# A list scheduler for a fused decoder layer: its step prices are taken from the trace, and steps on other rows than the one ahead get a price

## The chip, the core and the metric

The kernel runs on one core of a Trainium2 chip. A core has five engines with a queue each: TensorE (PE in the profile; its weight loads are PEld), VectorE (DVE), ScalarE (ACT), GpSimd (POOL) and SyncE (SP). Each works its queue in order and waits at semaphores for the others. SBUF and PSUM are memories of 128 partitions ("rows" below); matmuls write PSUM, and ScalarE and VectorE empty it. The metric is the device time of one launch in microseconds, the median of several runs; lower is better.

## The reference

One decoder layer, batch 1, 2048 tokens, width 1024, float32. `h` is the RMS-normalized input; one projection of `h` feeds three branches and their gates.

```python
h = rms_norm(x, norm_g[l])
p = h @ w_in[l]                      # 7552 columns, split into 13 parts
y_a = rwkv7_mix(...) * silu(z_a)     # 8 heads x 64, delta-rule state
y_b = sliding_window_sink_attn(...) * silu(z_b)   # 8 q heads, 2 kv heads x 64, window 128
y_c = memory_cross_attn(...) * silu(z_c)          # 4 heads x 128 over 256 memory tokens
gates = sigmoid(p_gate)              # 3 x 1024 per token
merged = gates_a * (y_a @ w_proj_a) + gates_b * (y_b @ w_proj_b) + gates_c * (y_c @ w_proj_c)
x = x + merged @ w_out
```

The recurrence of branch A is, for each head and token, `S = S * w + (S a) b^T + v k^T` and `y = S r`.

## The kernel before, in words

The 2048 tokens are worked in four stages of 512 (`sb` 0 to 3). All wide products are made in three matmuls of split operands: each float32 operand is split into a high and a low part, and `gemm3` adds high x high, high x low and low x high (lines 457 to 459). A projection block of 128 columns (`proj`) is 8 such triples into one of two PSUM buffers `mm`; a product with a `w_proj` block is 4. The weights are split in stage 0 (lines 439 and 440), written to DRAM, and read back in the stages after (`wblock`).

In each stage two streams are woven together. One (`stream_r`) is branch A, in two groups of two head pairs. `rwkv_prep` makes the chunked operands of a pair (chunks of 64 tokens): decays by a scan (line 697), then many VectorE steps on 64 of the 128 rows, since the two heads of a pair lie on rows 0 to 63 and 64 to 127 (`EV`, `OD`; lines 728, 732, 737, 742), Gram matrices on TensorE (line 753) that VectorE masks (lines 760 and 761), and transposes (line 770). One step of GpSimd (line 724) fills a mask in between. `rwkv_inverse` inverts small triangular matrices on VectorE (lines 803 to 805, 31 times three steps). `rwkv_chain` walks the eight chunks: bursts of small matmuls (lines 866, 867, 874, 859, 881), and between them a copy (line 869), a scaling (878) and the state's update (882) on VectorE, and scaled copies of the state on ScalarE (872). The other stream (`stream_f`) holds branches C and B with their softmaxes (line 1102, an exponential with a running sum), the gates, and two of the three merges. The third merge, the next stage's normalized input and the output product follow.

The order of the instructions in each engine's queue isn't that of the program. When all instructions have been written, `order` hands them to a list scheduler. `Step` gives each instruction a price: `busy`, how long it holds its engine, and `dur`, how long until its result is there. `cost_PE`, `cost_ACT`, `cost_DVE`, `cost_POOL` and `cost_SP` (lines 95 to 132) work these out from the operands. `steps` finds what each step must wait for and gives it a rank, which is its place in the program with a few corrections (weights are moved up to 1000 ahead, steps that read PSUM 600 ahead, the steps of the inverse 500 back). `lay_out` then plays the program with these prices: each time, the engine that can start earliest takes, among its steps that are ready at that moment, the one of least rank. A step counts as ready a fixed allowance after its feeders' ends: for TensorE 200 ns in the recurrence and 600 ns elsewhere (`LAT`, lines 65 to 67). When TensorE's last step had another tile size than the full array, steps of the same size go first. The orders found are fixed as dependencies, and the chip's queues follow them. So the prices reach the chip only through the order of each queue; no arithmetic step is added or removed by them (ScalarE's table loads stand wherever its order changes the set of functions).

Small matmuls that belong together are tied by `together` and are offered as a group.

Of the kernel before, what the change touches and what calls it, by code (L numbers as in the profile page):

```python
# [55 lines left out]
class Step:  # L56


    def __init__(self, ins, masks):
        self.ins, self.eng = ins, NAMES[ins.engine]  # L60
        self.reads, self.writes = ([self.region(a.bass_ap, masks) for a in aps if getattr(a, "bass_ap", None) is not None]
                                   for aps in (ins.ins, ins.outs))
        self.reads, self.writes = ([r for r in l if r] for l in (self.reads, self.writes))
        self.before, self.after, self.opens, self.group, self.end = set(), [], [], [], None
        self.lat = LAT[self.eng]
        if self.eng == "PE" and not any(r[0].startswith(("Z_", "W_", "R_")) or r[0] in ("Z", "W", "R") for r in self.reads):
            self.lat = 600
        self.bytes = 512 * self.n((self.writes + self.reads)[0]) if self.is_dma() else 0
        getattr(self, "cost_" + ("SP" if self.bytes else self.eng))()

# [25 lines left out]
    def cost_PE(self):  # L96
        out, mov, w = self.writes[0], *self.reads[:2]
        n = self.n(out)
        self.tile = tuple(128 if r[3][0][1] > 64 else 64 if r[3][0][1] > 32 else 32 for r in (mov, out))
        self.dense = mov[5] == F32R  # L100
        if self.dense:
            self.busy = 14 + 0.424 * n
        elif self.ins.is_transpose:
            self.busy = 108 if self.tile[0] == 128 else 55
        elif self.tile[1] == 128:
            self.busy = 223 + max(0, n - 128) * 1.7 if self.tile[0] == 128 else 62 + max(0, n - 64) * 0.8
        else:
            self.busy = 32 if self.tile[1] == 32 else max(58, 0.86 * n)
        self.dur = max(270, self.busy + 160)

    def cost_ACT(self):
        r = self.reads[0]
        self.dur = (170 if r[4] else 206) + 0.83 * self.n(r) + 90 * (len(self.reads) - 1 + len(self.writes) - 1)
        self.busy = self.dur - (85 if len(self.writes) > 1 else 38 if r[4] else -12)
        self.table = {AF.Sin: 1, AF.Exp: 2, AF.Tanh: 2}.get(self.ins.func, 0)

    def cost_DVE(self):
        r, two = self.reads[0] if self.reads else self.writes[0], sum(self.n(x) > 1 for x in self.reads) > 1
        slow = two or r[4] or type(self.ins).__name__ not in ("InstTensorScalarPtr", "InstTensorCopy", "InstMemset")
        self.dur = 155 + (1.05 if slow else 0.53) * self.n(r) + 30 * (len(self.reads) - 1)  # L120
        self.busy = max(100, self.dur - 85)
        if two and r[4] and self.n(r) <= 128:
            self.busy = self.dur + 20

    def cost_POOL(self):
        n = self.n(self.writes[0])
# [54 lines left out]
def lay_out(tc, todo):  # L181

    metas = {tag: meta.bufs for p in tc.info.pools if p.space != bass.MemoryType.DRAM for tag, meta in p.tag_meta.items()}
    source = {t.name: t.source_name for t in tc.info.tiles}
    tags = {tag: Tag(b) for tag, b in metas.items()}
    users, opened = {}, set()
    for s in todo:
        for name in {r[0] for r in s.reads + s.writes}:
            users.setdefault(name, []).append(s)
        for r in s.writes:  # L190
            if source[r[0]] in tags and r[0] not in opened:
                opened.add(r[0])
                s.opens.append(r[0])
                tags[source[r[0]]].queue.append(r[0])
    left = {name: len(u) for name, u in users.items()}
    heads = {tag: 0 for tag in tags}
    clock = {e: 0.0 for e in NAMES.values()}
    ready, parked = {e: {} for e in clock}, set()
    orders = {e: [] for e in clock}
    missing = {s: len(s.before) for s in todo}  # L200

    def seen_by(s, b):

        if b.eng == s.eng:
            return 0 if s.eng == "PE" else b.end + 30
        return b.end + s.lat

    def room(s):

        at, taken = 0.0, {}  # L210
        for name in s.opens + [n for g in s.group for n in g.opens]:
            tag = source[name]
            t, i = tags[tag], taken.get(tag, 0)
            if t.queue[heads[tag] + i] != name or len(t.free) <= i:
                return None
            taken[tag] = i + 1
            old = t.free[i]
            if old:
                at = max([at] + [seen_by(s, b) for b in last[old].values()])
        return at  # L220

    def offer(s):
        at = room(s)
        if at is None:
            parked.add(s)
            ready[s.eng].pop(s, None)
        else:
            parked.discard(s)
            ready[s.eng][s] = max([at] + [seen_by(s, b) for b in s.before])

    last = {name: {} for name in users}
    for s in todo:
        if not missing[s]:
            offer(s)
    tile, fp32, wires, table = (128, 128), False, 0, 2
    for _ in todo:
        best = None
        for e, rs in ready.items():
            if rs:
                at = max(clock[e], min(rs.values()))  # L240
                if best is None or at < best[0]:
                    best = at, e
        at, e = best
        can = [s for s, t in ready[e].items() if t <= at]
        s = min(can, key=lambda s: s.rank)
        if e == "PE":
            if tile != (128, 128) and s.tile != tile:
                s = min(can, key=lambda s: (s.tile != tile, s.dense, s.rank))
            if s.tile != tile:
                at += 95  # L250
            clock[e] = at + s.busy
            if s.dense and fp32:
                clock[e] += 95
            elif s.tile != tile and s.tile[1] < 128:
                clock[e] += 49
            tile, fp32 = s.tile, not s.dense
        else:
            if e == "ACT" and not s.bytes and s.table and s.table != table:
                at, table = at + 1280, s.table
            clock[e] = at + s.busy  # L260
        s.end = at + s.dur
        if s.bytes:
            wires = s.end = max(wires, s.end) + s.bytes / 330
        del ready[e][s]
        orders[e].append(s)
        again = set()
        for name in s.opens:
            tag = source[name]
            tags[tag].free.pop(0)
            heads[tag] += 1  # L270
            again.add(tag)
        for name in {r[0] for r in s.reads + s.writes}:
            if e not in last[name] or last[name][e].end < s.end:
                last[name][e] = s
            left[name] -= 1
            if not left[name] and source[name] in tags:
                tags[source[name]].free.append(name)
                again.add(source[name])
        for a in s.after:
            missing[a] -= 1  # L280
            if not missing[a]:
                offer(a)
        if again:
            for a in [a for rs in (parked, *ready.values()) for a in rs if any(source[n] in again for g in [a, *a.group] for n in g.opens)]:
                offer(a)
    return orders


def order(tc, manual, groups):

    orders = lay_out(tc, steps(list(tc.nc.cur_bb.bb.instructions), manual, groups))
    how = mybir.DependencyInfo(mybir.DependencyClass.NoSync, mybir.DependencyReason.DATA)
    for l in orders.values():
        for a, b in zip(l, l[1:]):
            tc.add_manual_dep(b.ins, a.ins.name, how, reason="order")
# [1083 lines left out]
```

## Time and profile before

| | |
|---|---|
| median of 3 runs | 2248.6 us (2247.82 to 2249.54) |
| profiled execution: its own time | 2250.41 us |
| profiled execution: span on the core | 2248.6 us |
| granted TensorE clock, mean | 0.998 |
| instructions in the trace | 36877 |
| TensorE busy | 2219.2 us, 99% |
| VectorE busy | 1531.7 us, 68% |
| ScalarE busy | 926.1 us, 41% |
| GpSimd busy | 149.7 us, 7% |
| DMA | 430.55 MB, mean 191 GB/s |

The span runs from the first to the last instruction of the program. A row of a group ("x1888 | 750.0, 397 | 1.5 <-DVE gt L928 1.5") gives the number of instructions, their busy time in microseconds, the mean length of one in nanoseconds, the engine's idle time just ahead of them, and who ended it. A row of the timeline gives start, length (of all, where several are merged), engine, line, operation, output and inputs, and in brackets the idle time ahead. Matmuls overlap, so the distance between two starts tells their pace, and not their length. Steps of ScalarE and VectorE overlap a little too: the next one often starts before the last has ended.

### The profile page before, as it was taken

Reading aid. Unit: us, or ns where it says so; the run is one execution under the profiler, and the core shown is the slowest. Engines: PE = TensorE matmul, PEld = TensorE weight load, DVE = VectorE, ACT = ScalarE, POOL = GpSimd, SP = SyncE. Lnnn points to the kernel's source line nnn. Section 1 sums busy time; section 2 is a strip of 40 time slices with the busy share of each in tenths; the row PEclk is TensorE's granted clock in tenths of the full one; section 3 lists DMA queues with packets and bytes.
Section 4 is the critical chain, followed back from the end, with each engine's and each line's share of the span. In section 5 each row is a group of like instructions: output and inputs, shape, how many; then the busy total and the mean of one; then the engine's idle time right before and its main releaser. Section 6 shows DMA issues by size and latency. Waiting matters only on the chain.

```text
span 2248.6 us, 36877 instructions
## 1 busy us (share of the span) xinstructions
PE 2219.2 (99%) x13706; PEld 1804.8 (80%) x13706; DVE 1531.7 (68%) x3951; ACT 926.1 (41%) x2024; POOL 149.7 (7%) x209
## 2 busy tenths in 40 slices
PE   8999999999999999999999999999999999999999
PEld 7887778778888778878888878787878887787887
DVE  6799699775479777953437957985245895896312
ACT  6664565545253354423214345442223435434210
POOL 2000010000000011000000001000000001100000
PEclk9999999999999999999999999999999999999999
DMA  6767556679944444447774434445675444343655
GB/s 215 271 232 245 191 188 220 221 269 353 324 146 160 134 141 150 147 165 235 239 239 136 164 122 150 148 135 195 229 250 199 157 142 160 115 148 132 206 191 193
DMA packets 146226, 430.55 MB, mean 191 GB/s; under 512 B 16640, under 2 KB 21120, under 8 KB 146048
## 3 DMA queue, kind: packets, MB, share of 16 engines
q1 hardware_dynamic: 129920, 398.83, 52.4%
q10 hardware_dynamic: 16128, 29.37, 4.0%
q8 instruction: 109, 1.79, 0.3%
q14 instruction: 69, 0.57, 0.1%
HBM read 333.24 MB, written 94.90 MB: 190 GB/s over the span
## 4 chain that ended last, share of the span: by engine, by line
PE 73%; DVE 18%; ACT 3%; DMA 2%; issue 2%; POOL 1%; SPq 0%; ACTq 0%; DVEq 0%; POOLq 0%
PE mm L457 18%; PE mm L459 18%; PE mm L458 17%; DVE ibc L803 2%; DVE ibc L804 1%; PE rw L881 1%; DVE Yi L805 1%; PE mm L1172 1%; PE mm L1173 1%; PE mm L1174 1%; ACT g L1102 1%; PE oo L1003 1%; DVE whl L440 1%; PE rw L866 1%; PE rw L874 1%
## 5 line engine op out<-in xcount | busy, mean ns | idle before, releaser
L457 PE MATMUL mm<-hH,whl 128*128 128x512 f32 x1888 | 750.0, 397 | 1.5 <-DVE gt L928 1.5
L459 PE MATMUL mm<-hH,whl 128*128 128x512 f32 x1888 | 748.3, 396 | 0.0
L458 PE MATMUL mm<-hL,whl 128*128 128x512 f32 x1888 | 748.0, 396 | 0.0
L457 PEld LDWEIGHTS mm<-hH,whl 128*128 128x128 f32 x1888 | 354.8, 188 | 72.7 <-DVE gt L928 1.9
L459 PEld LDWEIGHTS mm<-hH,whl 128*128 128x128 f32 x1888 | 354.8, 188 | 69.7
L458 PEld LDWEIGHTS mm<-hL,whl 128*128 128x128 f32 x1888 | 355.0, 188 | 67.8 <-issue 0.5
L439 ACT ACTIVATE whl<-raw 128x512 fp32r<-128x512 f32 x178 | 111.1, 629 | 144.8 <-PE mm L459 89.7
L440 DVE TENSOR_TENSOR whl<-raw,whl 128x512 fp32r<-128x512 f32 x178 | 123.3, 696 | 52.3 <-ACT whl L439 51.5
L457 PE MATMUL mm<-yh,whl 128*128 128x512 f32 x384 | 151.5, 395 | 1.4 <-DVE gt L1155 0.8
L459 PE MATMUL mm<-yh,whl 128*128 128x512 f32 x384 | 150.8, 393 | 0.0
L458 PE MATMUL mm<-yl,whl 128*128 128x512 f32 x384 | 150.7, 392 | 0.0
L872 ACT ACTIVATE SP<-Z,Pl 64x64 f32<-64x64 f32 x256 | 88.3, 345 | 112.7 <-DVE Z L882 109.2
L803 DVE STREAM_SHUFFLE ibc<-Nc 128x496 f32<-128x496 f32 (+30 forms) x248 | 113.3, 472 | 0.1
L1155 DVE SCALAR_TENSOR_TENSOR g<-g,mm 128x512 f32<-128x512 f32 x32 | 21.8, 680 | 128.6 <-PE mm L459 128.5
L804 DVE TENSOR_TENSOR ibc<-ibc,Yi 128x496 f32<-128x496 f32 (+30 forms) x248 | 104.4, 421 | 4.0
L805 DVE TENSOR_TENSOR Yi<-Yi,ibc 128x496 f32<-128x496 f32 (+30 forms) x248 | 102.9, 415 | 0.9
L1140 ACT ACTIVATE gt<-mm 128x512 f32<-128x512 f32 x64 | 38.0, 594 | 145.3 <-PE mm L459 145.1
L882 DVE SCALAR_TENSOR_TENSOR Z<-rw,Pl,SP 64x64 f32<-64x64 f32 x224 | 63.5, 283 | 50.0 <-PE rw L881 46.4
L457 PEld LDWEIGHTS mm<-yh,whl 128*128 128x128 f32 x384 | 72.1, 188 | 17.3 <-DVE g L1155 1.5
L459 PEld LDWEIGHTS mm<-yh,whl 128*128 128x128 f32 x384 | 72.1, 188 | 14.9
L458 PEld LDWEIGHTS mm<-yl,whl 128*128 128x128 f32 x384 | 72.1, 188 | 14.1
L1102 ACT ACTIVATE g<-g,mxs,st 128x256 f32<-128x256 f32 (+1 forms) x128 | 74.5, 584 | 18.8 <-DVE mxs L1095 18.6
(1812 smaller groups left out, 3786.7 us busy)
## 6 DMA issues: line engine op xcount, KB each, us to landing
whl<-k SPq DMA_DIRECT2D x486, 512.0 KB, 3.4
k<-whl SPq DMA_DIRECT2D x162, 512.0 KB, 4.3
raw<-in_w_in SPq DMA_DIRECT2D x118, 256.0 KB, 3.3
g<-in_x ACTq DMA_DIRECT2D x32, 256.0 KB, 4.4
out<-g ACTq DMA_DIRECT2D x32, 256.0 KB, 4.9
raw<-in_w_proj SPq DMA_DIRECT2D x24, 256.0 KB, 3.1
rt<-in_x ACTq DMA_DIRECT2D x24, 256.0 KB, 5.2
rt<-in_xt ACTq DMA_DIRECT2D x24, 256.0 KB, 5.8
```

The costliest lines, as they stand in the source:

```text
L439: S.activation(w[:, 0], raw, AF.Copy)
L440: V.tensor_tensor(w[:, 1], raw, w[:, 0].bitcast(F32), op=ALU.subtract)
L457: PE.matmul(out, lh, rh, start=i == 0, stop=False)
L458: PE.matmul(out, lh, rl, start=False, stop=False)
L459: PE.matmul(out, ll, rh, start=False, stop=i == n - 1)
L803: V.stream_shuffle(bc[:, :, :w], N_[:, :, s + 1:], [s] * 32)
L804: V.tensor_tensor(bc[:, :, :w], bc[:, :, :w], Y[:, :, s:s + 1].to_broadcast([128, n, w]), op=ALU.mult)
L805: V.tensor_tensor(Y[:, :, s + 1:], Y[:, :, s + 1:], bc[:, :, :w], op=ALU.add)
L872: S.activation(SP[h, i], Z[h, i, e, c], AF.Copy, scale=g[4][h, c:c + 1])
L882: upds = [V.scalar_tensor_tensor(Sst[h, g[0]] if c == NC_ - 1 else Z[h, i, e, c + 1], pS[h, i, e], g[4][h, c:c + 1], SP[h, i], op0=ALU.mul ...
L1102: S.activation(prs[b][:, i, m0:], prs[b][:, i, m0:], AF.Exp, scale=r2[:, b, i:i + 1], bias=mx[:, b, i:i + 1], accum_out=mx[:, b, 2 + i:3 + i])
L1140: S.activation(t, gp, AF.Tanh, scale=0.5)
```

## The change

The prices in `Step` and `lay_out` are other numbers, partly with other terms. The steps themselves, their dependencies, ranks and allowances are the same.

- TensorE: small corrections of the prices. A dense step behind an fp32 one is charged only where the tile size changes; a change of tile size costs 205, 150 or 140 ns (to a dense, a full-size fp32, a small step), where it was 95 ahead of the step and 95 or 49 more behind it.
- ScalarE: `busy` is `dur` less 97 ns for all steps (less 15 with a running sum), where it was `dur` plus 12, less 38 or less 85.
- VectorE: `dur` counts 60 ns for each narrow operand, the scan has a fixed 1225 ns, shuffles and transposes get 40 ns more; `busy` is `dur` less 83 ns, at least 70.
- New: each step notes the first row of its output and the highest first row among its operands (`rows`). Where this pair differs from that of the step ahead on VectorE or ScalarE, the step starts 105 ns later in the plan.
- `seen_by` has an added term that is 0 for all engines.

```diff
+        outs = [a.bass_ap for l in (ins.outs, ins.ins) for a in l if getattr(a, "bass_ap", None) is not None]
+        rows = [a.offset // math.prod(list(a.tensor.shape)[1:]) for a in outs[:1] + [a.bass_ap for a in ins.ins if getattr(a, "bass_ap", None) is not None]]
+        self.rows = rows[0], max(rows)
...
-            self.busy = 14 + 0.424 * n
+            self.busy = 15 + 0.4167 * n
         elif self.ins.is_transpose:
-            self.busy = 108 if self.tile[0] == 128 else 55
+            self.busy = 112 if self.tile[0] == 128 else 55
         elif self.tile[1] == 128:
-            self.busy = 223 + max(0, n - 128) * 1.7 if self.tile[0] == 128 else 62 + max(0, n - 64) * 0.8
+            self.busy = 221 + max(0, n - 128) * 1.64 if self.tile[0] == 128 else 66 + max(0, n - 64) * 0.75
         else:
-            self.busy = 32 if self.tile[1] == 32 else max(58, 0.86 * n)
+            self.busy = 32 if self.tile[1] == 32 else max(60, 0.88 * n)
...
-        self.dur = (170 if r[4] else 206) + 0.83 * self.n(r) + 90 * (len(self.reads) - 1 + len(self.writes) - 1)
-        self.busy = self.dur - (85 if len(self.writes) > 1 else 38 if r[4] else -12)
+        self.dur = (170 if r[4] else 206) + 0.83 * self.n(r) + 90 * (len(self.reads) - 1)
+        self.busy = self.dur - (15 if len(self.writes) > 1 else 97)
...
-        self.dur = 155 + (1.05 if slow else 0.53) * self.n(r) + 30 * (len(self.reads) - 1)
-        self.busy = max(100, self.dur - 85)
-        if two and r[4] and self.n(r) <= 128:
-            self.busy = self.dur + 20
+        self.dur = 152 + (1.042 if slow else 0.52) * self.n(r) + 60 * (len(self.reads) - max(wide, 1))
+        if "Scan" in kind:
+            self.dur = 1225
+        elif kind in ("InstStreamShuffle", "InstStreamTranspose"):
+            self.dur += 40
+        self.busy = max(70, self.dur - 83)
...
-        return b.end + s.lat
+        return b.end + s.lat + (0 if s.eng == "PE" else 0)
...
+            clock[e] = at + s.busy
             if s.tile != tile:
-                at += 95
-            clock[e] = at + s.busy
-            if s.dense and fp32:
-                clock[e] += 95
-            elif s.tile != tile and s.tile[1] < 128:
-                clock[e] += 49
-            tile, fp32 = s.tile, not s.dense
+                at += 97
+                clock[e] += 205 if s.dense else 150 if s.tile == (128, 128) else 140
+            tile = s.tile
...
+            if s.rows != rows[e] and e in ("DVE", "ACT") and not s.bytes:
+                at += 105
+                rows[e] = s.rows
             clock[e] = at + s.busy
```

More of the change, by code (lines that the diff above doesn't have):

```diff
@@ L112, in cost_ACT @@
         r = self.reads[0]
-        self.dur = (170 if r[4] else 206) + 0.83 * self.n(r) + 90 * (len(self.reads) - 1 + len(self.writes) - 1)
-        self.busy = self.dur - (85 if len(self.writes) > 1 else 38 if r[4] else -12)
+        self.dur = (170 if r[4] else 206) + 0.83 * self.n(r) + 90 * (len(self.reads) - 1)
+        self.busy = self.dur - (15 if len(self.writes) > 1 else 97)
         self.table = {AF.Sin: 1, AF.Exp: 2, AF.Tanh: 2}.get(self.ins.func, 0)
     def cost_DVE(self):
-        r, two = self.reads[0] if self.reads else self.writes[0], sum(self.n(x) > 1 for x in self.reads) > 1
-        slow = two or r[4] or type(self.ins).__name__ not in ("InstTensorScalarPtr", "InstTensorCopy", "InstMemset")
-        self.dur = 155 + (1.05 if slow else 0.53) * self.n(r) + 30 * (len(self.reads) - 1)
-        self.busy = max(100, self.dur - 85)
-        if two and r[4] and self.n(r) <= 128:
-            self.busy = self.dur + 20
+        r, wide = self.reads[0] if self.reads else self.writes[0], sum(self.n(x) > 1 for x in self.reads)
+        kind = type(self.ins).__name__
+        slow = wide > 1 or r[4] or kind not in ("InstTensorScalarPtr", "InstTensorCopy", "InstMemset")
+        self.dur = 152 + (1.042 if slow else 0.52) * self.n(r) + 60 * (len(self.reads) - max(wide, 1))
[4 more added lines that the diff above has]
+        self.busy = max(70, self.dur - 83)
     def cost_POOL(self):
@@ L234, in lay_out @@
             offer(s)
-    tile, fp32, wires, table = (128, 128), False, 0, 2
+    tile, wires, table = (128, 128), 0, 2
+    rows = {e: (0, 0) for e in clock}
     for _ in todo:
```

## The prediction, made before the change was run

> **What bounds the kernel now.** I read the page first, then the stretches by stage, the list of waits of TensorE, and at last the timeline around the waits. The busy shares and the shares of the chain that ended last come from the page:
>
> ```profile
> span 2248.6 us, 36877 instructions
> PE 2219.2 (99%) x13706; PEld 1804.8 (80%) x13706; DVE 1531.7 (68%) x3951; ACT 926.1 (41%) x2024; POOL 149.7 (7%) x209
> PE 73%; DVE 18%; ACT 3%; DMA 2%; issue 2%; POOL 1%; SPq 0%; ACTq 0%; DVEq 0%; POOLq 0%
> ```
>
> TensorE (PE) is busy for 2219.2 of 2248.6 us, VectorE (DVE) and ScalarE (ACT) for 68% and 41%. Whether the matmuls themselves run at their pace is seen in the starts, since their ends are modelled:
>
> ```profile
> 1001.40 0.40 PE L458 MATMUL mm<-hL,whl 128*128 128x512 f32 x1
> ...
> 1005.94 0.39 PE L457 MATMUL mm<-hH,whl 128*128 128x512 f32 x1
> ...
> 2244.59 0.39 PE L1174 MATMUL as__21887<-whl,mB 128*128 128x512 f32 x1
> ```
>
> Between the first two rows lie 20 steps of wide matmuls back to back: 4.54 us / 20 = 0.227 us each. The last row is the last matmul; it ends at 2244.98, so 3.6 us of the span are the tail behind PE (last addition and store). The change touches neither the number of matmuls nor their pace. What it can move is the order, and through it PE's idle time and its changes between wide and small matmuls. The idle time by stretch (start, stage 0, 1, 2, and 3 with the tail), each row giving length and PE's busy time:
>
> ```profile
> 0.00:31.00 31.00, 24.46 (x122) 21.19 (x123) 21.78 (x67) 18.89 (x45) 6.20 (x19) 0.83 0.61 197
> 31.00:593.00 562.00, 552.28 (x3456) 448.87 (x3455) 451.06 (x1082) 311.24 (x650) 43.76 (x55) 1.00 0.71 248
> 593.00:1139.00 546.00, 542.92 (x3360) 441.23 (x3358) 358.66 (x946) 203.50 (x453) 34.26 (x47) 1.00 0.53 177
> 1139.00:1686.00 547.00, 543.30 (x3359) 441.00 (x3358) 358.76 (x946) 203.61 (x453) 34.27 (x47) 1.00 0.53 175
> 1686.00:2248.60 562.60, 556.28 (x3416) 452.57 (x3416) 341.47 (x912) 188.88 (x424) 31.19 (x41) 1.00 0.49 164
> ```
>
> Behind the first 31 us PE is idle for 9.7 + 3.1 + 3.7 + 6.3 = 22.8 us, less the tail 19.2 us. That is all that a better order can win in waits: 0.85%. Whom PE waits for (microseconds, times, longest):
>
> ```profile
> PE rw L866 <- DVE Z L882: 2.3, 4, 1.4
> PE rw L770 <- DVE QE L761: 2.1, 3, 0.7
> PE rw L753 <- DVE whl L737: 1.8, 1, 1.8
> PE mm L457 <- DVE gt L928: 1.5, 1, 1.5
> PE rw L770 <- DVE whl L761: 1.3, 3, 0.5
> PE rw L881 <- DVE Z L878: 1.3, 4, 0.4
> PE rw L753 <- DVE QO L742: 0.8, 1, 0.8
> ```
>
> Nearly all are VectorE results that PE reached too early: the written order put the consumer ahead of the moment at which its data came. No wait of PE names a DMA.
>
> **The change part by part.** Nothing is computed otherwise; each engine's queue is written anew from other prices. So each price is held against the trace, before and after.
>
> *VectorE and ScalarE.* The rows are timelines of single engines; the difference of two starts is what a step really holds its engine for.
>
> ```profile
> 327.41 0.69 DVE L728 SCALAR_TENSOR_TENSOR whl<-rt,Pt 64x512 f32<-64x512 f32 x1
> 328.11 0.17 DVE L721 TENSOR_SCALAR dk<-rw 64x4 f32<-64x4 f32 x1
> ...
> 331.56 0.69 DVE L732 TENSOR_TENSOR whl<-rt 64x512 f32<-64x512 f32 x1
> 332.26 1.44 DVE L735 TENSOR_TENSOR rk__3604<-rk__3604,rt 128x512 f32<-128x512 f32 x1
> 333.62 0.68 DVE L574 TENSOR_TENSOR g<-g,cosT 128x512 f32<-128x512 f32 x1
> 334.23 0.68 DVE L440 TENSOR_TENSOR whl<-raw,whl 128x512 fp32r<-128x512 f32 x1
> ```
>
> ```profile
> 1886.08 1.42 ACT L872 ACTIVATE SP<-Z,Pl 64x64 f32<-64x64 f32 x4
> ...
> 1888.68 0.60 ACT L1120 ACTIVATE g<-as__18924 128x512 f32<-128x512 f32 x1 [0.47 <-PE as__18924 L1118]
> 1889.17 0.59 ACT L1120 ACTIVATE g<-as__18933 128x512 f32<-128x512 f32 x1
> ```
>
> ```profile
> L697 DVE TENSOR_TENSOR_SCAN rt<-smask,rt x16: 1217/1225/1226, 63.6 to 1952.4; 128x512 f32<-128x512 bf16 x16
> ```
>
> A full-width VectorE step with two inputs of 512: 0.61 us measured (333.62 to 334.23), 155 + 1.05 x 512 + 30 - 85 = 638 ns priced before, 152 + 1.042 x 512 - 83 = 603 after. The same on half the rows, with a step on other rows behind it: 0.70 measured (327.41 to 328.11), 638 before, 603 + 105 = 708 after. The scan lasts 1.225 us and was priced 723; after, 1225. A ScalarE copy out of PSUM: 0.49 measured (1888.68 to 1889.17), 557 before, 498 after. Four ScalarE steps on alternating halves take 1.42 us, so about 0.36 each; 361 before, 357 after. The new prices thus hit, and the old ones erred in two directions: too dear for full-width work (by 35 to 60 ns a step), too cheap for half-width VectorE work (by 62) and for the scan (by 502). One preparation of a head pair has 16 half-width VectorE steps (L728, L732, L737, L742, L760, L761) and one scan: 16 x 0.062 + 0.50 = 1.5 us too cheap, and just behind it stand the waits of L753 and L770, 0.4 to 1.8 us each, 1.8 + 0.8 + 2.1 + 1.3 = 6.0 us together.
>
> One part of these is not priced even now. In the rows above, L735 takes 1.44 us where its like takes 0.68, while GpSimd runs
>
> ```profile
> 331.61 1.55 POOL L724 TENSOR_TENSOR whl<-gmask,dk 128x512 f32<-128x512 bf16 x1 [34.65 <-DVE dk L722]
> ```
>
> That is 0.76 us of the 1.8 us wait at L753, which follows. I take 6.0 - 0.8 = 5.2 us as won here; the ends are 0 (the collision is all of it, a rival below) and 6.0.
>
> *TensorE.* Dense matmuls of 512 were priced 14 + 0.424 x 512 = 231.1 ns, after 228.4, against the 227 measured. Their number:
>
> ```profile
> L457 PE MATMUL mm<-hH,whl 128*128 128x512 f32 x1888 | 750.0, 397 | 1.5 <-DVE gt L928 1.5
> L457 PE MATMUL mm<-yh,whl 128*128 128x512 f32 x384 | 151.5, 395 | 1.4 <-DVE gt L1155 0.8 <-DVE g L1155 0.6
> ```
>
> Each of the two lines stands for three matmuls (hi-hi, hi-lo, lo-hi), so 3 x 2272 = 6816, and the old plan's PE was 6816 x 4.1 ns = 28 us slow over the run, more than all of PE's waits. The real PE runs ahead of the plan, until it meets a result that isn't there. After, it is 6816 x 1.4 ns = 9.5 us slow. Against this the change drops a price: a dense matmul behind a full-size fp32 one was charged 95 ns, now nothing unless the tile size changes. The trace shows the cost:
>
> ```profile
> 254.32 0.39 PE L881 MATMUL rw<-Z,whl 128*128 128x128 f32 x2
> ...
> 254.47 0.48 PE L458 MATMUL mm<-hL,whl 128*128 128x512 f32 x1
> 254.78 0.40 PE L459 MATMUL mm<-hH,whl 128*128 128x512 f32 x1
> ```
>
> 0.31 us to the next start instead of 0.227, so 85 ns. Counting only the 64 steps of the recurrence that end like this, 64 x 85 ns = 5.4 us are unpriced; the plan's PE is then at most 4 us slow, and perhaps a little fast, which errs on the side on which PE finds its data there. Prices for a change of tile size stay near the old ones (190 becomes 205 back to dense, 144 becomes 140 to a small tile), and they do not enter the choice of the next step; I take 0.
>
> Of the other 19.2 - 6.0 = 13.2 us of waits I take half, 6.6 us, as due to PE running ahead of its plan; the ends are 0 and 13.2. Against them stand new waits: the full-width steps lose the surplus that made their results come earlier than planned. What still covers them is the 600 ns (200 in the recurrence) that the plan adds ahead of each matmul, unchanged. I take 3 us, as much as stage 1 has now; the ends are 0 and the slow rival below.
>
> *The queues of SP and POOL* are ordered anew as well; their prices are unchanged. I cost this at nothing: no wait of PE is on a DMA, and weights may be asked for up to 1000 steps ahead. If this cover goes, each case costs at most a transfer's time to land.
>
> ```profile
> whl<-k SPq DMA_DIRECT2D x486, 512.0 KB, 3.4
> ```
>
> *Sum.* -5.2 - 6.6 + 3.0 = -8.8 us. The profiled execution took 2250.4 us (span 2248.6), 1.8 above the median of 2248.6. 2250.4 - 8.8 = 2241.6 for it, and 1.8 less for the median: 2240 (-0.4%). A difference under 0.2% (4.5 us) I call the same.
>
> **The rivals.**
> (A) *The waits at L753 and L770 are collisions with GpSimd, not wrong prices.* For it: L735 above. Against it: GpSimd's step runs once in a preparation, and it explains 0.76 of one 1.8 us wait. Then only 6.6 - 3.0 = 3.6 us go: 2245, the same. [...]
> (B) *Lost surplus, slower.* Place: the two PSUM buffers of the dense products. The products number 1888 / 8 + 384 / 4 = 332, and each can wait for the step that empties a buffer, as L457 does for L928 now (1.5 us). The surplus lost is 59 ns for ScalarE and 35 for VectorE, so about 0.1 us per pair of steps queued. To be slower the new waits must reach 5.2 + 6.6 + 4.5 = 16.3 us, that is 0.05 us for each product, or every fourth by 0.2 us. At 0.06 it is 20 - 11.8 = +8 us: 2257. Against it: the 600 ns of allowance.
> (C) *More changes of tile size, slower.* Results that arrive at other moments part small bursts that now follow one another. Its price:
>
> ```profile
> 999.66 0.40 PE L459 MATMUL mm<-hH,whl 128*128 128x512 f32 x1
> ...
> 999.99 0.33 PE L859 MATMUL yps<-Z,AB 64*64 64x64 f32 x4
> ...
> 1000.37 0.50 PE L457 MATMUL mm<-hH,whl 128*128 128x512 f32 x1
> ...
> 1000.70 0.39 PE L458 MATMUL mm<-hL,whl 128*128 128x512 f32 x1
> ```
>
> 0.33 us into the burst instead of 0.227, and 0.33 behind the first dense matmul: 0.2 us an excursion. It takes (8.8 + 4.5) / 0.2 = 66 more; at 80, 2240 + 16 = 2256. Against it: bursts are tied together, and the rule of choice is the same. [...]
>
> **How the numbers follow.** Forecast 0.53, A 0.15, B 0.20, C 0.12: faster 0.53, same 0.15, slower 0.32. The likeliest case alone spans 2229 (all 19.2 us gone) to 2246 (-5.2 + 3.0). The range of 8 in 10 goes on to the slow cases: down to 2228 (all idle gone and five excursions fewer), up to 2260 (B at 0.07 us a product: 23.2 - 11.8 = +11.4).
>
> **What would show it.** Right: PE's waits on L737, L742 and L761 all but gone, idle time behind 31 us at 10 to 12 us instead of 22.8 (tail included), busy time unchanged within 3 us. Wrong by B: new waits of L457 on L928, L1140, L1152 or L1155 in many places. Wrong by C: PE's busy time up with unchanged idle time. Wrong by A: L753 and L770 wait as before, beside L724. A wait of PE on a DMA would break the part on the queues.

## The result: 2242.7 us, a ratio of 0.9973

| | before | after |
|---|---|---|
| median | 2248.46 us (2247.77 to 2251.1, 9 runs) | 2242.7 us (2240.91 to 2246.05, 9 runs) |
| ratio, 95% interval | | 0.9973 (0.9963 to 0.9983) |
| profiled execution, span | 2250.4, 2248.6 us | 2242.7, 2240.9 us |

The changed kernel is 5.8 us faster in the median; the two profiled executions differ by 7.7 us, since that of before lay 1.9 us above its median. The line numbers of the changed kernel are 7 higher behind the changed functions: L464 to L466 are the three dense matmuls (457 to 459 before), L760 and L777 the Gram matrices and the transposes (753 and 770), L749 and L768 the VectorE steps ahead of them (742 and 761), L1179 the first output matmul (1172).

The page of the changed kernel, busy shares and the shares of the chain that ended last:

```profile
span 2240.9 us, 36879 instructions
PE 2216.9 (99%) x13706; PEld 1803.2 (80%) x13706; DVE 1533.1 (68%) x3951; ACT 926.8 (41%) x2024; POOL 149.4 (7%) x209
PE 72%; DVE 19%; ACT 3%; DMA 2%; issue 2%; POOL 1%; SPq 0%; ACTq 0%; DVEq 0%; POOLq 0%
```

To compare stages, both traces are cut where the first output matmul of each stage starts. The columns are start and end, length, and the busy time of each engine with its number of instructions. First the kernel before:

```profile
0.00:564.60 564.60, 548.35 (x3451) 446.53 (x3452) 454.31 (x1119) 319.63 (x677) 49.95 (x74) 0.99 0.70 241
564.60:1110.00 545.40, 542.32 (x3357) 440.98 (x3356) 367.58 (x960) 210.70 (x465) 34.26 (x47) 1.00 0.54 182
1110.00:1655.90 545.90, 542.84 (x3358) 440.90 (x3358) 358.44 (x946) 203.61 (x453) 34.27 (x47) 1.00 0.53 175
1655.90:2201.30 545.40, 542.07 (x3354) 440.59 (x3353) 343.62 (x917) 191.54 (x428) 31.19 (x41) 1.00 0.50 166
```

and the changed one:

```profile
0.00:562.50 562.50, 547.57 (x3451) 446.13 (x3452) 451.46 (x1118) 318.02 (x676) 48.60 (x74) 0.99 0.70 241
562.50:1106.20 543.70, 542.14 (x3357) 440.48 (x3356) 369.73 (x962) 212.57 (x467) 34.74 (x47) 1.00 0.53 184
1106.20:1649.90 543.70, 541.85 (x3357) 440.68 (x3356) 359.47 (x946) 204.18 (x453) 34.48 (x47) 1.00 0.52 176
1649.90:2193.50 543.60, 541.57 (x3354) 440.19 (x3354) 344.67 (x917) 191.36 (x427) 31.61 (x41) 1.00 0.50 167
```

TensorE does the same number of matmuls between the cuts, so the lengths compare. Stage 0 won 2.1 us, and the three others 1.7 + 2.2 + 1.8 = 5.7; what follows the last cut is 47.3 us before (2248.6 - 2201.3) and 47.4 after. The 2.1 us of stage 0 are not shown to be the change's: the profiled execution of before lay 1.9 us above its median, and the granted clock, the third number from the end of a row, differs. In the first 31 us it was 0.83 before, with 122 matmuls done, and after

```profile
0.00:31.00 31.00, 25.02 (x153) 22.22 (x153) 23.56 (x71) 20.24 (x48) 6.27 (x19) 0.94 0.66 208
```

while later in stage 0 it fell once more in the changed kernel alone (last section). In the three stages TensorE's idle time (length less busy) fell from 3.1 + 3.1 + 3.3 = 9.5 us to 1.6 + 1.9 + 2.0 = 5.4. TensorE's longest waits now:

```profile
PE rw L760 <- DVE QO L749: 2.7, 4, 1.1
PE rw L777 <- DVE QE L768: 2.4, 1, 2.4
...
PE mm L464 <- DVE mB L1159: 1.4, 1, 1.4
PE mm L1179 <- DVE g L1162: 1.0, 3, 0.4
PE rw L917 <- DVE rt L914: 0.9, 2, 0.6
PE rw L786 <- ACT BK L778: 0.8, 1, 0.8
PE mm L464 <- ACT gt L1147: 0.8, 1, 0.8
...
PE rw L873 <- DVE Z L889: 0.3, 1, 0.3
```

The waits in the recurrence (866 and 881 before, 2.3 and 1.3 us) are down to 0.3. The waits at the Gram matrices and the transposes, which the prediction expected to vanish, are 2.7 + 2.4 = 5.1 us where they were 6.0. Two new ones (L464 on L1159 and on L1147) are at the PSUM buffers of the dense products.

### The profile page after: what moved, and what is told of

Read it like the earlier page. It is cut to its first block, busy times and chain, and to the rows that moved or that the text cites. A ratio compares the mean times of both kernels' runs of the same rounds, so it can differ in the third digit from the quotient of the medians.

```text
span 2240.9 us, 36879 instructions
## 1 busy us (share of the span) xinstructions
PE 2216.9 (99%) x13706; PEld 1803.2 (80%) x13706; DVE 1533.1 (68%) x3951; ACT 926.8 (41%) x2024; POOL 149.4 (7%) x209
## 4 chain that ended last, share of the span: by engine, by line
PE 72%; DVE 19%; ACT 3%; DMA 2%; issue 2%; POOL 1%; SPq 0%; ACTq 0%; DVEq 0%; POOLq 0%
PE mm L464 17%; PE mm L465 17%; PE mm L466 17%; DVE whl L447 1%; PE mm L1179 1%; PE rw L888 1%; PE mm L1180 1%; PE mm L1181 1%; PE rw L873 1%; DVE ibc L810 1%; PE oo L1010 1%; PE rw L881 1%; DVE Yi L812 1%; DVE ibc L811 1%; PE yps L874 1%
## 5 line engine op out<-in xcount | busy, mean ns | idle before, releaser
L464 PE MATMUL mm<-hH,whl 128*128 128x512 f32 x1888 | 751.2, 398 | 1.4 <-DVE mB L1159 1.4
L466 PE MATMUL mm<-hH,whl 128*128 128x512 f32 x1888 | 747.0, 396 | 0.0
L464 PEld LDWEIGHTS mm<-hH,whl 128*128 128x128 f32 x1888 | 355.2, 188 | 73.6 <-DVE mB L1159 1.7
L466 PEld LDWEIGHTS mm<-hH,whl 128*128 128x128 f32 x1888 | 355.3, 188 | 68.8
L464 PE MATMUL mm<-yh,whl 128*128 128x512 f32 x384 | 151.3, 394 | 0.9 <-ACT gt L1147 0.8
L466 PE MATMUL mm<-yh,whl 128*128 128x512 f32 x384 | 151.6, 395 | 0.0
L464 PEld LDWEIGHTS mm<-yh,whl 128*128 128x128 f32 x384 | 72.1, 188 | 16.2 <-ACT gt L1147 1.0
L466 PEld LDWEIGHTS mm<-yh,whl 128*128 128x128 f32 x384 | 72.1, 188 | 14.7
L1147 ACT ACTIVATE gt<-mm 128x512 f32<-128x512 f32 x64 | 37.9, 592 | 105.5 <-PE mm L466 105.3
```

The source lines that it names most:

```text
L464: PE.matmul(out, lh, rh, start=i == 0, stop=False)
L466: PE.matmul(out, ll, rh, start=False, stop=i == n - 1)
L1147: S.activation(t, gp, AF.Tanh, scale=0.5)
```

## The experiments

Three theories were held against each other. *Hits*: the gain comes from VectorE and ScalarE prices that now meet the trace. *The plan's speed*: it comes from a TensorE that is no longer slower in the plan than on the chip, so that on the chip its data are there first; later widened to *the lead*: any edit that puts the feeders of TensorE further ahead in the order does it. *The lot*: any new order draws a new time, whatever the prices mean.

All runs were timed beside the kernel before. "Stage 0" is the start of the first output matmul, "stages 1 to 3" the time from there to that of stage 3, both from one profiled execution, which took 4.6 us more than its median in no_rows (2275.1) and 3.2 more in rows150 (2237.8).

| kernel | median us | ratio to before (95%) | stage 0 | stages 1 to 3 |
|---|---|---|---|---|
| before | 2248.5 to 2249.5 in four sets | 1 | 564.6 | 1636.7 |
| changed | 2242.7 | 0.9973 (0.9963 to 0.9983) | 562.5 | 1631.0 |
| only_vs | 2253.1 | 1.0019 (1.0010 to 1.0028) | 562.7 | 1641.0 |
| only_pe | 2248.2 | 0.9994 (0.9985 to 1.0002) | 567.3 | 1631.9 |
| jit_after | 2245.8 | 0.9987 (0.9978 to 0.9995) | 564.1 | 1631.7 |
| jit_before | 2246.1 | 0.9986 (0.9977 to 0.9995) | 562.2 | 1634.5 |
| dense231 | 2253.3 | 1.0016 (1.0007 to 1.0025) | 563.1 | 1640.1 |
| fp32_back | 2249.1 | 0.9999 (0.9990 to 1.0008) | 559.6 | 1639.6 |
| no_rows | 2270.5 | 1.0097 (1.0083 to 1.0111) | 564.9 | 1660.8 |
| dense218 | 2239.9 | 0.9959 (0.9947 to 0.9972) | 564.8 | 1625.8 |
| dense208 | 2244.8 | 0.9975 (0.9966 to 0.9985) | 573.3 | 1620.7 |
| allow200 | 2243.8 | 0.9974 (0.9964 to 0.9984) | 559.9 | 1634.2 |
| rows150 | 2234.7 | 0.9931 (0.9918 to 0.9945) | 566.3 | 1622.5 |
| noret_before | 2244.3 | 0.9975 (0.9965 to 0.9985) | 559.4 | 1635.4 |

The "plan's end" that some expectations name is where the scheduler's own clock of TensorE stands behind its last step.

Stage 0 needs a caution. In every profile the granted clock stands at half for a while in it, at the start and sometimes again later (the mean over the whole run is 0.996 to 0.999): 10.2 us in all before and in the changed kernel, 17.1 in only_pe, 6.8 in only_vs and noret_before, 3.4 in fp32_back, 13.7 in rows150 and dense208. Matmuls of 512 started every 0.43 us at half clock in the changed kernel, and every 0.227 us at full clock. By this estimate a microsecond at half clock costs half a microsecond where TensorE is busy, and up to 7 us of a difference in stage 0 can be the clock. In stages 1 to 3 the clock falls only in no_rows (twice) and dense218 (once), for 3.4 us each.

### Each half of the change alone, and two edits of no weight

The first half is the kernel before with the new `cost_ACT`, `cost_DVE` and `rows`; the second is the kernel before with the new `cost_PE` and the new charges for tile sizes.

> The kernel before with the new prices of VectorE and ScalarE and the new 105 ns for other rows; TensorE's prices are the old ones, so its dense matmul is priced 231 ns where 227 are measured. Theory of hits (the gain comes from VectorE's and ScalarE's prices): most of the gain is here, 2243 us. Theory of the plan's speed (the gain comes from a TensorE that is no longer slow in the plan): no gain, 2246 to 2252, with waits of TensorE as long as before. Theory of the lot (any new order draws a new time, prices or not): anywhere from 2238 to 2252.

> The kernel before with the new prices of TensorE alone. Theory of the plan's speed: all of the gain, 2242 us or less, idle time of TensorE behind 31 us at 18 us or less. Theory of hits: 2248, with waits at the half-width VectorE steps as before. Theory of the lot: 2238 to 2252.

```diff
 jit_after, of the changed kernel
-            self.busy = 15 + 0.4167 * n
+            self.busy = 15 + 0.4177 * n
 jit_before, of the kernel before
-            self.busy = 14 + 0.424 * n
+            self.busy = 14 + 0.423 * n
```

> The changed kernel with 0.4177 in place of 0.4167 ns a column for dense matmuls (0.5 ns in 228): a change of no weight for any theory of prices, which expect 2242 to 2244. Theory of the lot: it moves by 3 us or more, to either side.

> The kernel before with 0.423 in place of 0.424 ns a column for dense matmuls (0.5 ns in 231). Theory of hits: 2248. Theory of the plan's speed: an eighth of the 4 ns is taken back, 2247 to 2248. Theory of the lot: it moves by 3 us or more, to either side.

VectorE's and ScalarE's prices alone made the kernel slower, 2253.1 (1.0019). That is against the theory of hits, and 1 us outside what the plan's speed allowed. TensorE's prices alone gave no gain that can be told from none (0.9994), where the plan's speed expected 2242 or less. The stages tell the two apart. With the new VectorE and ScalarE prices alone, stages 1 to 3 (the last three rows of these) are longer than before:

```profile
0.00:562.70 562.70, 547.99 (x3451) 445.03 (x3452) 452.69 (x1120) 319.11 (x678) 48.87 (x74) 0.99 0.71 242
562.70:1109.10 546.40, 544.21 (x3357) 439.96 (x3356) 367.60 (x960) 210.55 (x464) 34.86 (x47) 1.00 0.54 181
1109.10:1656.40 547.30, 544.60 (x3358) 439.86 (x3358) 358.50 (x946) 203.96 (x453) 34.87 (x47) 1.00 0.53 175
1656.40:2203.70 547.30, 543.93 (x3354) 439.70 (x3353) 343.86 (x917) 191.86 (x428) 31.87 (x41) 1.00 0.50 165
```

With TensorE's alone they are as short as in the changed kernel, 1631.9 against 1631.0, but stage 0 is 2.7 us longer than before. So the gain in stages 1 to 3 goes with TensorE's prices. The 2.7 us of stage 0 are no more than the clock can explain: half of 17.1 - 10.2 us is 3.4.

Where only_vs loses is seen in the same rows. TensorE's idle time in stages 1 to 3 fell, from 9.5 us before to 2.2 + 2.7 + 3.4 = 8.3, and the waits at the Gram matrices and the transposes fell from 6.0 to 4.2 us in the whole run. Its busy time rose by 1.9 + 1.8 + 1.9 = 5.5 us. The starts in the trace show 94 changes of tile size a stage, against 95 before, so it is not more of those. As the length of a matmul is modelled (0.39 us at a pace of 0.227), delays shorter than the overlap count as busy; which steps they wait for was not traced.

The two edits of 0.5 ns moved the median by +3.1 us (of the changed kernel) and by -2.6 (of the kernel before, in its own set). That is the theory of the lot, and it is partly right: an order differs from the next by some 3 us that no price explains. A gain of 5.8 us is about twice that, and a single comparison of two orders says little about either price. The stages help again: jit_after keeps 1631.7 in stages 1 to 3 and loses in stage 0 (+1.6).

### Turning TensorE's price to both sides

```diff
 dense231, of the changed kernel (dense218: 5 + 0.4167 * n; dense208: -5 + 0.4167 * n)
-            self.busy = 15 + 0.4167 * n
+            self.busy = 14 + 0.424 * n
 fp32_back, of the changed kernel
+            elif s.dense and fp32:
+                clock[e] += 90
-            tile = s.tile
+            tile, fp32 = s.tile, not s.dense
 noret_before, of the kernel before
-            if s.dense and fp32:
+            if s.dense and fp32 and s.tile != tile:
```

> The changed kernel with the old price of a dense matmul, 231 ns (227 measured), and all else as changed. The plan's TensorE ends at 2245 instead of 2225 us. Theory of the plan's speed: the gain of the stages 1 to 3 (545.5 us each before, 543.7 after) goes back, 545 to 547 us a stage, 2247 to 2252 in all. Theory of hits (VectorE and ScalarE): 2242 to 2244. Theory of the lot: 2238 to 2250, with no rule in the stages.

> The changed kernel with 90 ns charged again for a dense matmul behind a full-size fp32 one (85 measured), so that every price is near its measured value; the plan's TensorE ends at 2243 us, near the chip's. Theory of hits: this is the most exact plan, at least as good as the changed kernel, 2238 to 2243. Theory of the plan's speed: the stages 1 to 3 lie between before and after, 544 to 545.5 us, 2243 to 2248 in all.

> The changed kernel with a dense matmul priced 218 ns, 9 ns less than measured, so that the plan's TensorE is far too fast and all its data come early; the plan ends at 2159 us. Theory of the plan's speed: fewer waits still, 542 to 543.5 us a stage, 2234 to 2241 in all. Theory of hits: prices off the mark cost, 2246 or more.

> The changed kernel with a dense matmul priced 208 ns (227 measured), twice as far below as in the kernel with 218. Theory of the lead (what counts is how far the plan's feeders run ahead of its TensorE, in any way): no worse than at 218, 2234 to 2241, stages 1 to 3 at 540 to 543 us. Rival (a price off the mark costs as much on this side, 218 was luck): 2244 or more.

> The kernel before without the 95 ns for a dense matmul behind a full-size fp32 one (85 measured), and nothing else changed; the plan's TensorE ends at 2239 instead of 2260 us. Theory of the plan's speed: this one edit gives a good part of the gain in the stages 1 to 3, 543.5 to 545 us each (545.5 before), 2242 to 2247 in all. Theory of hits: a price that was right is gone, 2249 or more.

With the new VectorE and ScalarE prices, stages 1 to 3 follow the price of a dense matmul step by step: 1640.1 at 231 ns, 1631.0 at 228, 1625.8 at 218 and 1620.7 at 208, against 227 measured. At 208 TensorE doesn't wait at all in stages 2 and 3 (539.29 busy of 539.30, 538.99 of 539.00), and stage 0 has grown to 573.3 us with 27 us of idle time:

```profile
0.00:573.30 573.30, 546.41 (x3450) 447.60 (x3451) 453.97 (x1114) 317.44 (x674) 49.29 (x74) 0.99 0.69 233
...
1115.70:1655.00 539.30, 539.29 (x3357) 441.79 (x3356) 360.14 (x946) 205.01 (x454) 36.18 (x47) 1.00 0.54 178
1655.00:2194.00 539.00, 538.99 (x3353) 441.35 (x3352) 344.53 (x917) 193.10 (x429) 33.22 (x41) 1.00 0.51 168
```

So 218 is faster than 208 in all (2239.9 against 2244.8): the lead is paid in stage 0, which has VectorE busy for 454 us of 573 against 360 of 539. The largest part of the idle time is one wait,

```profile
PE rw L760 <- DVE QO L749: 8.8, 1, 8.8
```

which ends at 317.6 us. VectorE was busy for 14.3 of the 15 us from 305 to 320, and from 311.2 to 321.5 the clock stood at half. That misses the expectation for 208 (no worse than at 218), and the total falls to the rival (2244 or more); stages 1 to 3 did what the lead says.

The most telling run is fp32_back. It puts back one price that the change dropped and that is right (90 ns charged, 85 measured). With every price near the trace the gain is gone: 2249.1, 0.9999. Both theories had expected better, hits 2238 to 2243 and the plan's speed 2243 to 2248. Its mark is in stages 1 to 3, which lose 8.6 us (1631.0 to 1639.6). The gain there hangs on a price that is *not* that of the trace. Taken away from the kernel before, with nothing else, the same price wins 5.3 us (2249.5 to 2244.3), but this is weaker evidence. It shows mostly in stage 0 (559.4), where the clock accounts for some 1.7 us, and stages 1 to 3 won 1.3 us, less than was expected and less than the 2.2 us that 0.5 ns won in jit_before.

### The price for other rows, and the lead by another road

```diff
 no_rows, of the changed kernel (rows150: 150)
-                at += 105
+                at += 0
 allow200, of fp32_back
-        return b.end + s.lat + (0 if s.eng == "PE" else 0)
+        return b.end + s.lat + (200 if s.eng == "PE" else 0)
```

> The changed kernel without the 105 ns for a step whose first rows differ from the one ahead; VectorE and ScalarE are then too fast in the plan at each change of halves (0.70 us measured, 603 ns priced). Theory of hits: waits of TensorE at the half-width steps return, 545 us or more a stage, 2246 to 2254. Theory of the plan's speed, where only TensorE's price counts: 2242 to 2245.

> The changed kernel with 150 in place of 105 ns for a step on other rows. Theory of the lead: VectorE's results come later in the plan than on the chip, which gives its readers more room; 2238 to 2244. Theory of hits: 105 is the measured value, and 150 costs about as much to the other side as the miss of 45 ns of 105 would of the 28 us that its loss costs, 2248 or more.

> The kernel with all prices near their measured values (the one that charges the return from fp32 again, 2249 us), with 200 ns more of allowance ahead of each matmul in the plan: 800 and 400 in place of 600 and 200 ns. Theory of the lead: the exact plan gains as the fast one does, 2239 to 2245, stages 1 to 3 at 544 us or less. Theory of the plan's speed alone (a TensorE that drifts behind the chip's is needed): 2247 to 2251, stages as in the exact plan, 546 to 547 us.

Without the 105 ns the changed kernel is the slowest of all, 2270.5 (1.0097): 27.8 us for this one price. Stages 1 to 3, with TensorE's busy time beside the length:

```profile
564.90:1118.00 553.10, 546.91 (x3358) 441.05 (x3358) 367.56 (x961) 212.42 (x466) 35.34 (x47) 1.00 0.54 180
1118.00:1670.50 552.50, 545.85 (x3357) 439.73 (x3356) 358.12 (x946) 204.41 (x453) 35.09 (x47) 1.00 0.53 173
1670.50:2225.70 555.20, 547.09 (x3354) 440.95 (x3353) 344.05 (x917) 191.62 (x427) 32.46 (x41) 1.00 0.50 163
```

Idle time is 6 to 8 us a stage, and busy time 4 to 5.5 us more. In stages 1 and 3 some 1.7 us of that is the clock at half (837.9 to 841.3 us and 1947.3 to 1950.7); the rest fits delays too short to count as idle. At 150 ns, some 50 above the 0.09 to 0.10 us that the trace shows (0.70 to 0.71 us from start to start where the rows change, 0.61 where they don't), the kernel is the fastest of all: 2234.7, 0.9931 (0.9918 to 0.9945), 8.0 us below the changed one:

```profile
566.30:1106.80 540.50, 539.68 (x3358) 441.49 (x3358) 368.03 (x963) 213.00 (x467) 37.26 (x47) 1.00 0.55 186
1106.80:1647.70 540.90, 539.68 (x3358) 441.55 (x3357) 357.64 (x947) 204.41 (x453) 36.95 (x47) 1.00 0.54 177
1647.70:2188.80 541.10, 539.46 (x3354) 441.05 (x3353) 342.64 (x917) 191.55 (x427) 34.12 (x41) 1.00 0.51 167
```

The theory of hits expected 2248 or more. And allow200, the exact plan with 200 ns more of allowance ahead of each matmul, is at 2243.8 where the exact plan is at 2249.1: the lead can be had without a wrong price. (In allow200 24 matmuls moved behind the first cut, so its first two entries in the table are shifted by some 5 us, and stages 1 to 3 compare as about 1629; stages 2 and 3 took 542.9 and 543.2 us.) Three roads (a faster TensorE, dearer row changes, a longer allowance) lead to the same place. That is as far as the runs settle it. Open is why the 150 ns do more than either of the others, and how much of its 8 us is the lot; it is one order, and no second one near 150 was run.

## Why the prediction was right, point by point

- **The sign and the size.** Forecast 2240 (-0.4%), measured 2242.7 (-0.27%), inside the range. The sum was -5.2 - 6.6 + 3.0; as measured it is +4.4 for VectorE's and ScalarE's prices (2248.7 to 2253.1) and -10.4 for TensorE's on top (2253.1 to 2242.7). The total came near because two terms were off in opposite directions, which is luck. The terms don't even add: TensorE's prices alone, on the kernel before, won 0.5 us in all, which can't be told from none, and 4.8 in stages 1 to 3.
- **"I take 6.0 - 0.8 = 5.2 us as won here"** is the step that failed. The waits at the Gram matrices and the transposes went from 6.0 to 5.1, and to 4.2 with these prices alone, which still cost 4.4 us in all. A likely reading is that the two errors of the old prices, full-width steps too dear and half-width ones too cheap, made up for each other, and that correcting both took away a surplus and gave no lead in its place. That no_rows loses 27.8 us, with full-width steps corrected and half-width ones still too cheap, fits it. But no run traces the loss of only_vs to a surplus that is gone, so this isn't shown. What was right is that the row price belongs to the set.
- **"6.6 us, as due to PE running ahead of its plan"** named the mechanism that carries the gain and was too small. Taking the dense price back alone costs 10.6 us (2242.7 to 2253.3).
- **The dropped 95 ns** were counted as a small thing that "errs on the side on which PE finds its data there". They are worth 6.4 us put back into the changed kernel, and 5.3 us dropped from the old one. The term was mis-sized: the prediction counted 64 such steps and 5.4 us, but in the trace of before 256 dense matmuls start right behind a full-size fp32 one, and 256 x 85 ns = 21.8 us. By that sum the new plan's TensorE isn't up to 4 us slow but 9.5 - 21.8, some 12 us fast. The plan's ends in the expectations agree: 2260 us before, where the chip's last matmul ends at 2245.0, and 2225 after, where it ends at 2237.3 (2240.9 less a tail of 3.6). So the plan went from 15 us slow to 12 us fast.
- **"new waits ... I take 3 us"**: the place was right (L464 on L1159 and L1147, 1.4 and 0.8 us). only_vs, with the new VectorE and ScalarE prices and the old ones of TensorE, is 4.4 us slower. That is the direction of rival B but not its sign, since TensorE's idle time fell there and no wait at the dense products is longer than 1.3 us. So B is neither shown nor ruled out; with TensorE's new prices no such loss is left.
- **Rival A**, that the waits of the Gram matrices are collisions, fits three of the five. In stage 1 of the changed kernel, on GpSimd, VectorE and TensorE:

```profile
830.39 1.38 POOL L731 TENSOR_TENSOR AB<-gmask,dk 128x512 f32<-128x512 bf16 x1 [0.81 <-DVE dk L729]
...
830.79 1.52 DVE L749 TENSOR_TENSOR QE<-rr__8782,Pt 64x512 f32<-64x512 f32 x1
...
835.77 0.34 PE L760 MATMUL rw<-QO,BK 64*128 64x128 f32 x1 [0.55 <-DVE QO L749]
```

  L749 takes 1.52 us where its like takes 0.69, and five steps later TensorE waits 0.55 us, less than the 0.83 lost; in stages 2 and 3 L749 takes 1.53 us at the same place. The kernel before shows it too: at 826.69 us L732 took 1.53 us beside GpSimd's L724 (826.30, 1.38 us), and at 828.84, with GpSimd idle, 0.69 us. What makes a step beside GpSimd's longer isn't shown: L739, which started at 830.24 us and overlaps the same L731, took 0.63 us. The long wait of 2.4 us at L777 in stage 0 is not of this kind: GpSimd has no instruction from 300 to 310 us. That it would leave the time the same was wrong.
- **Rival C**: TensorE's instructions are 13706 as before, and its busy time between the cuts fell by 0.2 to 1.0 us a stage, and the starts in its trace show 94 changes of tile size in each of stages 1 to 3 (95 before), so no excursions were added.
- **The queues**: still no wait of TensorE names a DMA.
- **The sign** for being right, idle time of 10 to 12 us behind 31 us, didn't come: it is 18.0 us (22.8 before), while busy time stayed within the 3 us named (2.3 less). More than half of the idle time that was to go stayed.
- **Not foreseen** was that stage 0 and the other stages answer differently, that the clock falls in stage 0, and that a change of 0.5 ns in a price moves the total by 3 us.

## What to carry to other kernels

In a list scheduler whose order is fixed before the run, a price isn't better because it is closer to the trace. In this kernel it counted more on which side it errs: orders were better with the busiest engine a little faster in the plan than on the chip (1640.1 us in stages 1 to 3 at 231 ns, 1620.7 at 208), or its feeders a little slower (1631.0 at 105 ns, 1622.5 at 150), since it loses time when it meets missing data and little when the data lie ready. The lead ends where the feeders are busy all the time themselves, as around the wait of 8.8 us in stage 0 at 208 ns (VectorE busy for 14.3 of 15 us). Correct prices together, then set the lead on purpose (an allowance, or a factor on one engine), and judge it by stage and over several near settings, because orders that differ by nothing of weight are 3 us apart here, and single executions of rows150 with a granted clock of 0.997 and 0.999 lie some 4 us apart.

## What the runs showed of the hardware

In stage 0 of the changed kernel the granted clock of TensorE fell to half behind 3.41 us in which TensorE was busy for 1.06 us. Its longest pause there was 2.41 us, the wait at L777 (TensorE's busy time is the second number, the granted clock the third from the end):

```profile
306.95:310.36 3.41, 1.06 (x8) 0.84 (x8) 3.36 (x6) 0.00 (x0) 0.00 (x0) 1.00 0.87 304
310.36:317.19 6.83, 5.98 (x20) 4.66 (x19) 6.39 (x19) 5.29 (x12) 0.00 (x0) 0.50 0.01 4
```

and the pace of matmuls of 512 in it, 0.43 us instead of 0.227:

```profile
313.37 0.63 PE L465 MATMUL mm<-hL,whl 128*128 128x512 f32 x1
313.80 0.63 PE L466 MATMUL mm<-hH,whl 128*128 128x512 f32 x1
314.23 0.63 PE L787 MATMUL rw<-rt,ones 128*128 128x512 f32 x1
```

From 310.4 to 317.2 us TensorE is busy for 5.98 us at half of its clock, so about 3.0 us are lost behind a longest pause of 2.4 us. The kernel before has a clock of 1.00 from 31 to 593 us; it lost more at the start (0.83 in the first 31 us). By this estimate the wait at L777 and the slow stretch behind it cost some 5 us, nearly as much as stages 1 to 3 won.

The falls in the first 31 us look alike. Before, TensorE was busy for 1.69 us from 10.84 to 14.25 us, and the clock stood at 0.50 from 14.25 to 24.49. In the changed kernel it was busy for 1.83 us from 13.40 to 16.82, and the clock stood at 0.50 from there to 20.23. In no_rows no wait of TensorE behind the start is longer than 1.9 us, and the clock fell twice in stages 1 to 3. Whether little use alone brings the clock down isn't settled. Before, TensorE was busy for 1.64 us from 333.80 to 337.21, and the clock stayed at 1.00. In rows150 4 us with 2.06 us busy (308 to 312) were followed by 4 us at 1.00, and the 4 us with 2.38 busy behind them (312 to 316) by 4 us at 0.54.

The mean clock also differs between executions of one kernel: in rows150 two took 2232.8 and 2233.6 us at a mean granted clock of 0.999, and two 2237.0 and 2237.8 at 0.997.
